# Branch a of a hybrid encoder block as a Strassen product, its operands' sums made beside the projections

## The chip, the cores and the metric

The kernel runs on one core of a Trainium2 chip, as one launch. The metric is device time in microseconds. A core has a matrix engine (PE, with its weight loads shown apart as PEld), a vector engine (DVE), a scalar engine (ACT), GpSimd (POOL) and SyncE (SP); here SP does nothing but issue transfers between DRAM and the core's memories. Each of these works its own list of instructions in order. PSUM is the memory that PE accumulates in; in attention eight banks of 128 x 512 numbers are shared out to fixed uses.

## The reference, cut to what matters

All is float32, with 1024 rows of x (S) and 1024 columns (D).

```
h  = rmsnorm(x);  proj = h @ w_in                      # q, k, v, f, g_b, g_c, hc, two gates
ya = g_b * causal_conv3(g_c * hc)                      # 1024 x 512
yb = softmax(q k^T / 8 + sums of log f, causal) v      # 8 heads of 64: 1024 x 512
ya_d = ya @ w_branch[0]                                # 1024 x 512 by 512 x 1024: "branch a"
yb_d = yb @ w_branch[1]                                # "branch b"
m  = (sigmoid(gate_conv) * ya_d + sigmoid(gate_attn) * yb_d) @ w_out
x  = x + rmsnorm(m);  then a SwiGLU FFN in the same manner
```

The change is to how `ya_d` is computed.

## The kernel before, in words

Every large product is computed in three passes (`mm3`): both operands are split into a high and a low part (`copy` makes the high part on ACT or DVE, `sub` the rest on DVE), and high x high, high x low and low x high are accumulated in PSUM. So one 128 x 128 by 128 x 512 block costs three matmuls. The large products besides branches a and b are already Strassen products: seven block products in place of eight, on sums of the blocks A11 to A22 and B11 to B22 that bear the names S1 to S4 and T1 to T4.

The program's stages, in order: the pre-norm and v (0 to 60 us), 18 projection jobs of 84 matmuls (jobs 0 to 3 make q and k, 4 to 9 what ya is made of, 10 to 17 the gates), attention, branch b, the output projection, the FFN and its down projection. `job` 17 is mixed with the first two steps of attention. In a projection job `strassen` (line 679) makes the seven products; a generator `steps` may be handed to it, and a piece of side work is then done at two places of the job. Before, the side work is `wo_steps`, which makes the sums of w_out's blocks in jobs 7 and 8 and 10 to 15 and spills them to DRAM.

Attention is a loop over steps t = 2 to 22. In each, PE computes scores of two head pairs' blocks (tile `sp`, `step_qk`), multiplies the probabilities of an earlier step with v (`po`, `pv_pair`), and turns probabilities into columns (`tps`, `turn_bank`, copied out as `ptT` by ACT and DVE). Between the two halves of `tps` stands a filler: pieces of branch a, in tile `pba`. Before, `branch_a(d, n)` (twelve matmuls in four units of three) computes the output block of 128 columns d and half n of the rows, and `units` says how many units of three a step gets: 2 in steps 6, 7, 11, 12, 19, 20, 4 in steps 8 to 10, 13 to 16, 21 and 22, 3 in step 17 and 1 in step 18, and none up to step 5. Three blocks of twelve are left for after step 22 (the "tail", 36 matmuls), before branch b (tile `pbb`). A block ends with a multiplication on DVE, `um<-sg,pba`, by its gate tile sg. The operands are w_branch's columns d (`load_wa`, 256 KB, tile `s`, split to `s4h` and `s4l` by `split_wa`) and quarters of ya (`load_ya`, `split_ya`, tiles `yh` and `yl`).

Within attention the program's order is kept on every engine (`strict[0] = engines`). A step's list of `cuts` (splits) is worked off in its middle; its list `at` (loads, divisions) stands at its end. All loads named here are issued by SP. Two chains of other work share SP's list. When the probabilities of a head pair are summed up, `inverse_rows` turns the inverse sums (PE `tr`, DVE copy `rT`), `ri_dram<-rT` stores them to DRAM and `rb<-ri_dram` reads them back spread over partitions, and `divide` multiplies yb by rb on DVE. For the last head pair this happens in two parts, in steps 19 and 22. And `load_kv` and `q_load` bring in the next head pair's k, v and q (tiles `lo`, `v`, `raw`) at the ends of steps 5 and 10; v's buffer is free when the step's `po` has read it.

All instructions of the helpers bear line 76 in the profile, so rows are told apart by their tiles.

## Time and profile before

| | us |
|---|---|
| median of three runs (lowest, highest) | 1316.39 (1316.14, 1318.62) |
| the profiled execution | 1316.02 |
| its span; mean granted clock of PE | 1313.9; 0.999 |
| PE busy | 1305.2 (99% of the span) |
| DVE, ACT, POOL busy | 920.8, 557.1, 188.2 |
| one projection job | 19.1 |
| attention, step 2 to the end of step 22 | 409.2 to 542.8 |
| branch a's tail | 542.8 to 551.1 |

The page gives the busy time of each engine, the span in 40 slices, and the chain of work that ended last. Where a stage of some microseconds matters, the timeline gives single rows: start, duration, engine, line, operation, and tiles (out<-in); SPq rows are the issues of transfers on SP's queue, and the time from issue to landing is listed apart. Steps of attention begin with `sp`: step 11 at 466.98, step 12 at 473.37, step 19 at 520.92, step 20 at 527.48, step 21 at 532.92 (its filler comes first there) and step 22 at 538.56 (likewise).

### The profile page before, as it was taken

How to read it: one execution, taken by the hardware profiler on the slowest of the kernel's cores; microseconds unless marked ns; L12 is line 12 of the kernel's file. 1: busy time of each engine (PE TensorE's matmuls, PEld its weight loads, DVE VectorE, ACT ScalarE, POOL GpSimd, SP SyncE). 2: the span in 40 equal slices, each digit the busy share in tenths (PEclk: the TensorE clock that was granted, in tenths of full speed). 3: DMA queues.
4: the chain of work that ended last, by engine and by line, in shares of the span. 5: the costliest groups of instructions: out<-in, count | busy, mean ns of one | idle time of the engine just before them, and what ended most of it. 6: DMA issues, size and time to landing. Idle time of an engine off the chain costs nothing.

```text
span 1313.9 us, 17693 instructions
## 1 busy us (share of the span) xinstructions
PE 1305.2 (99%) x6695; PEld 1086.7 (83%) x6695; DVE 920.8 (70%) x1314; ACT 557.1 (42%) x869; POOL 188.2 (14%) x349
## 2 busy tenths in 40 slices
PE   9999999999999999999999999999999999999998
PEld 8988888888888888888888888888888888888886
DVE  7885668776656876676677698866766666676674
ACT  7623223243445765613778332322232234444451
POOL 3110001021212221011222122111100110000001
PEclk9999999999999999999999999999999999999999
DMA  6353324565536445674476566533323337966451
GB/s 234 91 159 97 103 87 136 172 209 204 182 121 213 149 135 175 203 250 143 123 243 226 164 205 198 171 112 104 111 74 120 105 112 274 361 215 193 159 169 64
DMA packets 168533, 215.71 MB, mean 164 GB/s; under 512 B 11496, under 2 KB 113968, under 8 KB 168448
## 3 DMA queue, kind: packets, MB, share of 16 engines
q1 hardware_dynamic: 146480, 141.39, 34.4%
q0 software_dynamic: 21952, 73.19, 15.1%
q8 instruction: 52, 0.85, 0.3%
q14 instruction: 33, 0.27, 0.1%
q10 hardware_dynamic: 16, 0.00, 0.0%
HBM read 153.41 MB, written 61.15 MB: 163 GB/s over the span
## 4 chain that ended last, share of the span: by engine, by line
PE 98%; ACT 1%; DVE 1%; issue 0%; DVEq 0%; POOLq 0%; POOL 0%; ACTq 0%
PE b L76 62%; PE pd L76 16%; PE pv L76 3%; PE pbb L76 3%; PE pba L76 3%; PE po L76 2%; PE tps L76 2%; PE sp L76 2%; PE tp L76 1%; PE ma L76 1%; PE mb L76 1%; ACT pt L76 0%; PE spin L76 0%; ACT yh L76 0%; DVE um L76 0%
## 5 line engine op out<-in xcount | busy, mean ns | idle before, releaser
L76 DVE TENSOR_TENSOR c<-c,b 128x512 f32<-128x512 f32 x215 | 146.8, 683 | 95.0 <-PE b L76 87.1
L76 DVE TENSOR_TENSOR lo<-raw,hi 128x1024 fp32r<-128x1024 f32 (+1 forms) x91 | 109.6, 1205 | 78.7 <-PE b L76 63.0
L76 ACT ACTIVATE hi<-raw 128x1024 fp32r<-128x1024 f32 (+1 forms) x98 | 99.6, 1016 | 97.8 <-PE b L76 55.1
L76 ACT ACTIVATE hi<-sx 128x1024 fp32r<-128x1024 f32 x44 | 46.8, 1063 | 217.2 <-PE b L76 191.1
L76 DVE TENSOR_TENSOR lo<-sx,hi 128x1024 fp32r<-128x1024 f32 x44 | 53.8, 1223 | 41.7 <-PE b L76 40.5
L76 PE MATMUL b<-w12h,lo 128*128 128x512 f32 x208 | 80.9, 389 | 0.0
L76 PE MATMUL b<-w12h,hi 128*128 128x512 f32 x204 | 79.4, 389 | 0.0
L76 PE MATMUL b<-w12l,hi 128*128 128x512 f32 x204 | 79.4, 389 | 0.0
L76 PE MATMUL b<-hh,hi 128*128 128x512 f32 x176 | 68.9, 391 | 0.0
L76 PE MATMUL b<-hl,hi 128*128 128x512 f32 x176 | 68.6, 390 | 0.0
L76 PE MATMUL b<-hh,lo 128*128 128x512 f32 x176 | 68.5, 389 | 0.0
L76 DVE TENSOR_TENSOR sx<-raw 128x512 f32<-128x512 f32 x78 | 53.6, 688 | 20.5 <-DMA raw<-in_w_in_dram 12.0
L76 PE MATMUL b<-w,s4h 128*128 128x512 f32 x208 | 64.0, 389 | 0.0
L76 PE MATMUL pd<-hi,lo 128*128 128x512 f32 x160 | 62.2, 389 | 0.0
L76 PE MATMUL pd<-hi 128*128 128x512 f32 x160 | 61.9, 390 | 0.0
L76 PE MATMUL pd<-ghi 128*128 128x512 f32 x148 | 57.6, 389 | 0.0
L76 PE MATMUL pd<-ghi,glo 128*128 128x512 f32 x148 | 57.6, 389 | 0.0
L76 PE MATMUL pd<-glo,ghi 128*128 128x512 f32 x148 | 57.6, 389 | 0.0
L76 POOL DMA_DIRECT2D a_dramA<-um x33 | 17.9, 541 | 276.1 <-DVE um L76 275.5
L76 PE MATMUL b<-hT34h,lo 128*128 128x512 f32 x136 | 52.9, 389 | 0.0
L76 PE MATMUL b<-hT12h,hi 128*128 128x512 f32 x136 | 52.9, 389 | 0.0
L76 PE MATMUL b<-hT12l,hi 128*128 128x512 f32 x136 | 52.9, 389 | 0.0
(457 smaller groups left out, 3576.4 us busy)
## 6 DMA issues: line engine op xcount, KB each, us to landing
raw<-in_w_gate_up_dram SPq DMA_DIRECT2D x52, 512.0 KB, 3.7
raw<-in_w_in_dram SPq DMA_DIRECT2D x35, 512.0 KB, 3.8
a_dramS<-um POOLq DMA_DIRECT2D x44, 256.0 KB, 3.0
a_dramA<-um POOLq DMA_DIRECT2D x33, 256.0 KB, 2.6
sg<-sg_dram SPq DMA_DIRECT2D x32, 256.0 KB, 4.7
graw<-a_dramS SPq DMA_DIRECT2D x14, 512.0 KB, 4.3
sg_dram<-c POOLq DMA_DIRECT2D x24, 256.0 KB, 2.3
raw<-in_w_down_dram SPq DMA_DIRECT2D x11, 512.0 KB, 4.8
```

Of the source, the lines that this page charges most:

```text
L76: ins = getattr(self.engine, name)(*args, **kw)
```

## The change

Branch a becomes a Strassen product of 2 x 2 blocks (512 x 512 columns and rows of the output, contracted over 2 x 256). Each of its seven products P1 to P7 is made in four pieces p of 128 columns; a piece is two blocks deep, six matmuls (`a_chunk`): 28 pieces, 168 matmuls instead of 192. One piece is done in each step 2 to 20 and in step 22, two in step 21 (P5 of p = 3 and P6 of p = 0), and six after step 22: P6 of p = 1, 2, 3 and P7 of p = 1, 2, 3. P1 and P2 of a p share one PSUM accumulation, as do P3 and P4, and P6 and P7 share theirs; when each piece is done DVE (for P1 it is a copy) adds it to a quarter of um, and multiplies a finished quarter by its gate.

The operands' sums (S1 to S4 of the weights, T1 to T4 of ya) and the high and low parts of all operands are made in `wa_steps` and `ya_steps`, as side work of projection jobs 2 to 5 and 10 to 15, and stored by POOL to `wa_dram` and `ya_ops`. In attention they are loaded as they are used, without a split: the weights of each piece (256 KB, one per step in order of use, a ring of five buffers, at the end of a step) and seven operands of ya (1 MB each, in the four homes `HOME`). The loads of k, q and the bias of the first head pair move from job 12 to job 16.

```diff
+    wa_dram = dpool.tile([7, P, 2, 2, NC], F32, name="wa_dram")
+    ya_ops = dpool.tile([7, P, 2, 2, NC], F32, name="ya_ops")
...
+    SUMS_W = ("S3", "S2", "S1", "S4", "A11", "A12", "A22")
+    SUMS_Y = ("T1", "T3", "T2", "T4", "B21", "B22", "B11")
...
+    def wa_steps(k):
...
+        def out(op, t):
+            n = t.shape[1]
+            h = half_tile(w0_tile(tags.popleft()))[:, :n]
+            copy(h, t)
+            strict[0] = ("vector",)
+            sub(t.bitcast(F32R), t, f32(h))
+            strict[0] = ()
+            nc.gpsimd.dma_start(of(op, n)(0), f32(h))
+            nc.gpsimd.dma_start(of(op, n)(1), t)
...
+        sub(s4_[:, 0], a[:, 0], a[:, 1])
+        add(u4[:, 0], a[:, 1], b[:, 1])
+        sub(s4_[:, 1], u4[:, 0], a[:, 0])
+        sub(u4[:, 1], b[:, 0], s4_[:, 1])
+        strict[0] = ()
+        yield
+        out(0, s)
+        yield
+        out(2, u)
...
+    def ya_steps(k):
...
+        sub(t[:, 0], a[:, 1], a[:, 0])
+        sub(u[:, 0], b[:, 1], t[:, 0])
+        strict[0] = ()
+        yield
+        strict[0] = ("vector",)
+        sub(t[:, 1], b[:, 1], a[:, 1])
+        sub(u[:, 1], b[:, 0], u[:, 0])
+        strict[0] = ()
+        yield
+        out(4, b)
+        out(6, a[:, :1])
+        if k == 0:
+            load_rows(ya_rows(1))
+        yield
+        out(0, t)
+        yield
+        out(2, u)
...
+    plans = defaultdict(lambda: [[], []])
+    for first, make in (
+        (((2, 0), (2, 1), (3, 0), (3, 1)), lambda: wa_steps(0)),
+        (((4, 0), (4, 1), (5, 0), (5, 1)), lambda: wa_steps(1)),
+        (((10, 1), (11, 0), (11, 1), (12, 0), (12, 1)), lambda: ya_steps(0)),
+        (((13, 0), (13, 1), (14, 0), (14, 1), (15, 0)), lambda: ya_steps(1)),
+        *(
+            (((j, 0), (j, 1), (j + 1, 0), (j + 1, 1)), lambda k=k: wo_steps(k))
+            for k, j in enumerate((7, 10, 12, 14))
+        ),
+    ):
+        it = make()
+        for j, n in first:
+            plans[j][n].append(it)
...
+            if ij == 16:
...
+                steps=job_steps(plans.pop(ij)) if ij in plans else None,
...
+    HOME = dict(B11="h0", B21="l0", T2="h1", T3="l1", T4="h0", T1="h1", B22="l1")
+    wring = deque()
+
+    def load_y(o):
+        yops[o] = yq.tile([P, 2, 2, NC], F32R, tag=f"y{HOME[o]}", name=f"y{o}", bufs=1)
+        nc.sync.dma_start(f32(yops[o]), ya_ops[SUMS_Y.index(o)])
+
+    def load_w(o, p):
+        if not wring:
+            wring.extend(("s4", "s4h", "s4h", "s4l", "s4l"))
+        tag = wring.popleft()
+        wops[o, p] = wtile(tag, 1 if tag == "s4" else 2, F32R, (P, 4, P))
         nc.sync.dma_start(
-            was[d], w_branch[0, 0][:, d * P : (d + 1) * P].rearrange("(k p) m -> p k m", p=P)
+            f32(wops[o, p]),
+            wa_dram[SUMS_W.index(o)][:, :, :, p * P : (p + 1) * P].rearrange(
+                "p t k c -> p (t k) c"
+            ),
...
+    SEQ = dict(
+        P1=("A11", "B11"), P2=("A12", "B21"), P3=("S2", "T2"), P4=("S3", "T3"),
+        P5=("A22", "T4"), P6=("S1", "T1"), P7=("S4", "B22"),
+    )
+    OPENS = ("P1", "P3", "P5", "P6")
...
+        w, y = SEQ[what]
+        w, y = wops.pop((w, p)), yops[y]
+        kw = {} if what in OPENS else dict(skip_group_check=True)
+        for k in range(2):
             mm3(
-                ps, (wh[:, k, :], wl[:, k, :]), (ya2[n][0][:, k, :], ya2[n][1][:, k, :]),
-                k == 0, k == 3,
+                ps, (w[:, k], w[:, 2 + k]), (y[:, 0, k], y[:, 1, k]),
+                what in OPENS and k == 0, k == 1, **kw,
             )
-            yield None if k < 3 else lambda: mul(um[:, d, ns], sgs[d, n], ps)
-
-
-    FILL = [(d, n) for n in range(2) for d in range(2)]
-    FILL += [(d, n) for d in range(2, 6) for n in range(2)] + [(6, 0)]
-
-    def filler():
-        for d, n in FILL[:-2]:
-            yield from branch_a(d, n, pst, "mb")
-        for d, n in FILL[-2:]:
-            yield from branch_a(d, n, pss, "S")
+        c11, c12, c21, c22 = a_quarters(p)
+
+        def drain():
+            if what == "P1":
+                copy(c21, ps)
+            elif what == "P2":
+                mul(c11, sgs[2 * p, 0], ps)
+            elif what == "P3":
+                add(c12, c21, ps)
+            elif what == "P4":
+                add(c22, c21, ps)
+            elif what == "P5":
+                add(c21, c22, ps)
+                if p < 3:
+                    gate(2 * p + 1, 0)
+            elif what == "P6":
+                add(c22, c22, ps)
+                if p < 3:
+                    gate(2 * p + 1, 1)
+            else:
+                add(c12, c12, ps)
+                gate(2 * p, 1)
...
+    chunks = defaultdict(list)
+    for t, what, p in (
+        (2, "P1", 0), (3, "P2", 0), (4, "P1", 1), (5, "P2", 1), (6, "P1", 2), (7, "P2", 2),
+        (8, "P1", 3), (9, "P2", 3), (10, "P3", 0), (11, "P4", 0), (12, "P5", 0),
+        (13, "P3", 1), (14, "P4", 1), (15, "P3", 2), (16, "P4", 2), (17, "P3", 3),
+        (18, "P4", 3), (19, "P5", 1), (20, "P5", 2), (21, "P5", 3), (21, "P6", 0),
+        (22, "P7", 0),
+    ):
+        chunks[t].append((what, p, pss if what in ("P6", "P7") else pst, "S" if what in ("P6", "P7") else "mb"))
+    A_TAIL = [("P6", 1), ("P6", 2), ("P6", 3), ("P7", 1), ("P7", 2), ("P7", 3)]
+    w_order = deque(
+        (SEQ[what][0], p)
+        for what, p in [c[:2] for t in sorted(chunks) for c in chunks[t]] + A_TAIL
+    )
...
+    for t in range(2, 23):
+        at[t].append(next_w)
+    at[21].append(next_w)
+    for t, o in ((6, "T2"), (7, "T3"), (10, "T4"), (19, "T1"), (19, "B22")):
+        at[t].append(do(load_y, o))
+    for t in (6, 8, 10, 13, 14, 20, 21, 22):
+        at[t].append(next_sg)
...
+    load_y("B11")
+    next_w()
     load_kv(1)
     q_load(1)
+    load_y("B21")
+    for _ in range(2):
+        next_w()
+    for _ in range(4):
+        next_sg()
...
+    done = []
+    for n, (what, p) in enumerate(A_TAIL):
+        done.append(a_chunk(what, p, psm, "mm"))
+        if w_order:
+            next_w()
+        if n < 2:
+            yb_split(0, (2 * n, 2 * n + 1))
+        if n == 2:
+            for m in done[:2]:
+                m()
+            for x in range(2):
+                next_sg()```

On SP, around the end of step 10, the order is now as follows (`s4h` and `s4l` are buffers of the weights' ring, `wa_dram` and `ya_ops` the spilled operands; `yT_4484` is T4):

```order
L76 DMA cb<-c_dram 128x1024 x2
L76 DMA lo<-qk_dram_69 128x1024
L76 DMA v<-v_dram 128x8x128
L76 DMA raw<-qk_dram_69 128x1024
L76 DMA s4h<-wa_dram 128x4x128
L76 DMA yT_4484<-ya_ops 128x2048
L76 DMA sg<-sg_dram_140 128x512
```

T4 and a piece's weights stand behind the loads of the next head pair, where before a raw piece of w_branch and two gate tiles stood. From step 19 on SP had before:

```order
L76 DMA ri_dram_129<-rT 4x128 x2
L76 DMA raw<-in_w_out_dram 128x2x512
L76 DMA rb<-ri_dram_129 64x512 x2
L76 DMA s_5240<-in_w_branch_dram 128x4x128
L76 DMA sg<-sg_dram_140 128x512 x2
L76 DMA raw<-in_w_out_dram 128x2x512
L76 DMA ri_dram_129<-rT 4x128 x2
L76 DMA sg<-sg_dram_133 128x512
L76 DMA rb<-ri_dram_129 64x512 x2
L76 DMA sg<-sg_dram_134 128x512
```

The same stretch of SP in the changed program, from the first `rb` on (`s_5245` are the weights of P6, p = 0, `yT_5247` is T1, `yB_5249` is B22, the `s4l` behind the second `rb` the weights of P6, p = 3):

```order
L76 DMA rb<-ri_dram_131 64x512 x2
L76 DMA s_5245<-wa_dram 128x4x128
L76 DMA yT_5247<-ya_ops 128x2048
L76 DMA yB_5249<-ya_ops 128x2048
...
L76 DMA raw<-in_w_out_dram 128x2x512
L76 DMA ri_dram_131<-rT 4x128 x2
L76 DMA rb<-ri_dram_131 64x512 x2
L76 DMA s4l<-wa_dram 128x4x128
L76 DMA sg<-sg_dram_140 128x512
L76 DMA s_5439<-wa_dram 128x4x128
L76 DMA s4h<-wa_dram 128x4x128 x2
```

The first `rb` now has the operands of P6 behind it, and the second the weights of P6 of p = 3 and of all of P7 that is left. On PE the end of attention is now, from step 20's second half on:

```order
L76 MATMUL pba<-yT_4484,s4l 128x512 x6
L76 MATMUL tps<-ident,pt 128x128 x6
L76 MATMUL pba<-yT_4484,s4l 128x512 x6
L76 MATMUL pba<-yT_5247,s_5245 128x512 x6
L76 MATMUL po<-ptT,v 64x128 x12
L76 MATMUL tps<-ident,rows_970 128x128 x10
L76 MATMUL pba<-yB_5249,s4h 128x512 x6
L76 MATMUL tr<-ident,ri 8x128
L76 MATMUL po<-ptT,v 64x128 x10
L76 MATMUL pba<-yT_5247,s4h 128x512 x6
L76 MATMUL pba<-yT_5247,s4l 128x512 x12
```

Twelve matmuls stood before in the place of step 22's six (`yB_5249`); the last row is P6 of p = 2 and of p = 3.

170 lines of the change are left out of this document (102 added, 68 removed).

## The prediction

> **What bounds the kernel now.** I read the page first (busy times, slices, chain), then the busy time by stage, the waits of TensorE in attention, and last the rows of the SP queue beside the rows of PE and DVE at the places where the change puts loads.
>
> ```profile
> PE 1305.2 (99%) x6695; PEld 1086.7 (83%) x6695; DVE 920.8 (70%) x1314; ACT 557.1 (42%) x869; POOL 188.2 (14%) x349
> GB/s 234 91 159 97 103 87 136 172 209 204 182 121 213 149 135 175 203 250 143 123 243 226 164 205 198 171 112 104 111 74 120 105 112 274 361 215 193 159 169 64
> PE 98%; ACT 1%; DVE 1%; issue 0%; DVEq 0%; POOLq 0%; POOL 0%; ACTq 0%
> ```
>
> PE sets the time: 1305.2 of 1313.9 us are busy, and 98% of the chain is PE. So a matmul that goes is time gained, and anything that makes PE wait is time lost. By stage (the columns are PE, PEld, DVE, ACT and POOL busy, clock, DMA share, GB/s):
>
> ```profile
> 200.00:300.00 100.00, 100.00 (x443) 82.81 (x442) 74.24 (x103) 35.03 (x43) 13.50 (x25) 1.00 0.52 173
> 155.90:175.00 19.10, 19.10 (x87) 15.73 (x86) 13.78 (x21) 5.64 (x7) 0.55 (x1) 1.00 0.35 112
> 308.60:327.70 19.10, 19.10 (x86) 15.83 (x85) 14.52 (x20) 8.53 (x11) 4.87 (x9) 1.00 0.64 225
> 409.20:429.47 20.27, 20.27 (x235) 16.82 (x234) 14.99 (x38) 17.30 (x43) 6.06 (x15) 1.00 0.68 241
> 442.93:479.93 37.00, 36.51 (x339) 30.23 (x339) 26.76 (x59) 24.18 (x57) 7.99 (x18) 1.00 0.40 129
> 532.92:551.13 18.21, 18.21 (x118) 14.66 (x117) 11.55 (x19) 9.49 (x16) 1.56 (x2) 1.00 0.61 197
> ```
>
> The second and third rows are projection jobs, the others attention (steps 2 to 5, 8 to 12, then step 21 to the end of branch a). PE is nowhere idle for long, and DVE has room in all of them.
>
> **The change part by part.**
>
> *Matmuls.* Branch a had 8 x 2 x 4 x 3 = 192 of them and now has 28 x 6 = 168, so 24 go. The row of 387 ns that the tile view gives for one is not its price, since matmuls overlap; their starts are.
>
> ```profile
> 543.17 0.39 PE L76 MATMUL pba<-yl,s4h 128*128 128x512 f32 x1
> 547.05 0.39 PE L76 MATMUL pba<-yh,s4h 128*128 128x512 f32 x1
> ```
>
> These two are 17 matmuls apart: 3.88 us, 0.228 us each (the first stage row gives 100/443 = 0.226). 24 x 0.228 = **-5.5 us**. By place: steps 2 to 5 gain six each (24 more), steps 8 to 10, 13 to 16 and 22 lose six each (48 fewer), step 17 loses three and step 18 gains three. The 36 after the last step stay. So 18 of the 24 (-4.1 us) go before step 22, six (-1.4 us) in it.
>
> *Splits in attention.* 16 subtractions on DVE (0.68 us each) and 16 copies on ACT (0.62) go with the splitting of wa and ya; 16 multiplications of um on DVE become 36 operations. DVE then has four more in all, spread over 21 steps, below its room. What PE can gain is bounded by its waits for ACT and DVE there:
>
> ```profile
> PEld po L76 <- ACT ptT L76: 0.9, 2, 0.6
> PEld po L76 <- ACT pt L76: 0.6, 2, 0.4
> PEld tps L76 <- ACT rows L76: 0.6, 2, 0.4
> PEld tps L76 <- ACT pt L76: 0.4, 2, 0.3
> PEld pba L76 <- DVE um L76: 0.4, 1, 0.4
> ```
>
> The five sum to 2.9 us. Most stand in steps 6 to 8, whose splits go, so at most about 2.3 and at least 0 is won: I take a little more than the middle, **-1.5 us**.
>
> *Sums beside the projections.* 18 half jobs get additions, subtractions and splits on DVE, some 28.6 us in all (7.3 us for each half of wa, 7.0 for each half of ya, worked out from 0.68 us for 128x512 and 1.22 for 128x1024), and 32 stores on POOL. A projection job has 19.1 us of PE and DVE is busy 13.8 and 14.5 in the two quoted. It gets some 3 to 4 more per job: 17.5 to 18. The stored 14.7 MB spread over 10 jobs (190 us) are 77 GB/s more, on 112 to 225 there; a slice of the page moves 361. I cost it at **0**; what hides it is PE's 19.1 us per job, and without that cover it is 0.5 us for each of ten jobs, 5 us (a rival below).
>
> *Loads in attention.* Before, 4 MB of wa and ya came in; now 7 MB of wa sums (28 of 256 KB) and 7 MB of ya sums (7 of 1 MB). The amount is no problem at 129 to 241 GB/s, but all of them are issued by SP, which works its queue in order, and three stand behind an issue that has to wait. That is where I expect the loss.
>
> *T4, for P5(0) in step 12.* As the order rows show, it is behind v and raw of the next head pair.
>
> ```profile
> 470.19 0.37 SPq L76 DMA_DIRECT2D v<-v_dram  x1
> 470.61 1.62 SPq L76 DMA_DIRECT2D raw<-qk_dram  x1
> DMA to landing us min/median/max: 6.5/6.5/6.5
> ...
> 477.59 0.48 PE L76 MATMUL pba<-yh,s4h 128*128 128x512 f32 x1
> ```
>
> The v load went out at 470.19, 3.2 us into step 11 (its buffer is read by PE's po of that step), raw at 470.61, and raw took 6.5 us (third row), to 477.1. Step 12's filler is reached at 477.59. T4 is issued after raw and the weights, at about 473, and has 1 MB behind raw's 512 KB: with 6.5 to 8 us it lands at 479.5 to 481, with the 4.9 of a row below it is in time within 0.3. I take 479.6: **+2.0 us** (0 to 3.5).
>
> *T1, for P6(0) in step 21.* It is issued in step 19, behind the load of rb, and rb's buffers are read by the divisions of yb on DVE.
>
> ```profile
> 529.19 1.28 DVE L76 TENSOR_TENSOR yb<-yb,rb 128x512 f32<-128x512 f32 x2
> 530.51 1.09 SPq L76 DMA_DIRECT2D rb<-ri_dram  x2
> 533.59 0.68 DVE L76 TENSOR_TENSOR s4l<-s,s4h 128x512 fp32r<-128x512 f32 x1
> 534.19 0.68 DVE L76 TENSOR_TENSOR um<-sg,pba 128x512 f32<-128x512 f32 x1
> 534.39 0.40 PE L76 MATMUL pba<-yh,s4h 128*128 128x512 f32 x1
> wh<-wt_dram SPq DMA_DIRECT2D x1, 1024.0 KB, 4.9
> w<-w_dram POOLq DMA_DIRECT2D x2, 1024.0 KB, 6.6
> ```
>
> rb goes out at 530.51, when both divisions are done. The change puts P5(1)'s addition and gate ahead of them on DVE (0.6 us each, from 533.59 to 534.19): 531.7. Then rb takes 1.09 and the weights of P6(0) 0.5, so T1 goes out at 533.3. A transfer of 1 MB lands in 4.9 to 6.6 us; with 5.7 that is 539.0. PE reaches P6(0) at 534.39, the seventh filler matmul of step 21. **+4.6 us** (2.6 without the delay on DVE and with 4.9; 6 at the other end). Queued behind it on PE are po and tps of that step, so all of what follows is late by as much.
>
> The Trainium skill ("DMA: Bandwidth & Descriptors", section "Anatomy of one DMA — SWDGE (gpsimd) path") fits a DMA's time as 2.0 us plus bytes over 436 GB/s, for GpSimd's path. By that estimate 1 MB takes 4.4 us, T1's wait is 3.3 and the whole sum 1323.5 us instead of 1324.8; the two rows above are longer and I go by them.
>
> *The weights of P6(3), after step 22.* They are issued in step 22 behind the way of the row sums of the last head pair: PE's tr, DVE's rT, the store ri_dram, and its reading back as rb.
>
> ```profile
> 538.56 0.48 PE L76 MATMUL pba<-yh,s4h 128*128 128x512 f32 x1
> 541.40 0.68 DVE L76 TENSOR_TENSOR s4l<-s,s4h 128x512 fp32r<-128x512 f32 x1
> 543.13 0.27 DVE L76 COPY rT<-tr 8x128 f32<-8x128 f32 x1
> 543.43 0.60 SPq L76 DMA_DIRECT2D ri_dram<-rT  x2
> 546.67 1.09 SPq L76 DMA_DIRECT2D rb<-ri_dram  x2
> 547.85 4.55 SPq L76 DMA_DIRECT2D sg<-sg_dram  x3
> SPq L76 <- DMA ri_dram<-rT: 6.5, 4, 3.3
> s<-in_w_branch_dram SPq DMA_DIRECT2D x8, 256.0 KB, 4.5
> DMA to landing us min/median/max: 2.8/2.8/2.8
> ```
>
> SP stores at 543.43, waits for the store until 546.67 (the row of waits has it as its longest, 3.3 us), issues rb, and is free at 547.85. Now DVE has two more operations of um ahead of rT and one s4l less, +0.6: SP is free at 548.4, 9.85 us after step 22 began (538.56). 256 KB land in 2.8 us at best (last row, the s of 534.30) and 4.5 at the median; with the load of rb still going I take 5.0: 14.85 after the step's start. The 24 matmuls from P6(3) on take 24 x 0.228 = 5.5, so branch a ends 20.3 us after the step's start, where it ended 551.13 - 538.56 = 12.57 after it: **+7.8 us** net, the six matmuls saved in step 22 already in it (5.6 with 2.8 us, 9.9 at 7). Without the weights being late P6(3) would be reached 5.6 us after the step's start, so the wait itself is 9.2 us. Two shorter waits ahead of it (step 21's rows behind P5(3)'s addition, P6(1) behind the addition of P7(0), which holds its PSUM bank) are swallowed by it. Branch b behind it has its operands earlier, counted from its own start, so nothing follows from there.
>
> The same section of the Trainium skill says that DMA engines do not wait on semaphores, the issuing sequencer does, before it dispatches. That speaks against this change, and the trace agrees: SP issued nothing from 544.5 to 546.67.
>
> *Sum.* -4.1 - 1.5 + 0 + 2.0 + 4.6 + 7.8 = +8.8 us. The profiled execution lasted 1316.0 us (span 1313.9 and 2.1 around it), 0.4 below the median of the runs: 1316.0 + 8.8 = **1324.8 us**. The low ends give -4.1 - 2.3 + 2.6 + 5.6 = +1.8 (1317.8), the high ends -4.1 + 3.5 + 6 + 9.9 = +15.3 (1331).
>
> **Rivals.**
>
> *The loads are in time (faster).* If SP's waits end early enough, as when rb no longer holds the loads up, or the loads land before PE comes, only the gain is left: -5.5 - 1.5 = -7.0, 1309.0 us. For it speaks that PE hardly waits for DMA before; against it that T1 would have to land 1.1 us after its issue at 533.3, and P6(3)'s weights before they are issued. It decides if both are issued over 5 us earlier than I read. 0.10.
>
> *One late load, not three (no change).* If the last load is in time but T4 and T1 are late, -5.5 - 1.5 + 2.0 + 4.6 = -0.4 (1315.6); if only the last is late, -5.5 - 1.5 + 9.2 = +2.2 (1318.2). For it: each price hangs on one place in a queue. 0.12.
>
> *The sums stall the projections too (slower still).* Two jobs of DVE at 18 us of 19.1 leave 1 us; if c's accumulations are late behind a block of sums, PSUM banks are not free and PE waits 0.5 us in ten jobs: 1329.8 us. Against it: no wait of PE in the projections before. 0.13.
>
> My own forecast has the rest, 0.65, with a range of its own of 1317.8 to 1331.
>
> **How the numbers follow.** A measurement can tell about 0.2% (2.6 us) from no change. Faster is the first rival, 0.10, and a little of the second; the second's two cases lie within 2.6 us, and so does the low edge of my forecast; the rest is slower. Faster 0.11, same 0.13, slower 0.76. The range is 1316.5 to 1331.5: it takes in both bounds of the sum, one case of the second rival and the third rival, and leaves out the first rival and the other.
>
> **What would show it.** Between step 2 and step 20 PE should take 4.1 us less, but for a wait of some 2 us ahead of pba in step 12, put down to the 1 MB yT. In step 21 PE should stand some 4 to 5 us between the sixth and the seventh filler matmul, for the second 1 MB yT, issued right behind rb. After step 22 PE should stand about 9 us ahead of the third chunk of the tail, for weights issued right behind the last rb. The projection jobs should still take 19.1 us with DVE at 15 to 18. If PE has no wait over 2 us in step 21 and after step 22, the forecast is wrong and the time is near 1309; if the projections grow, the third rival holds.

## The result and the profile after

The changed kernel takes 1355.69 us (median of four runs, 1352.99 to 1356.86), the kernel before beside it 1316.79 (four runs, 1316.14 to 1318.62): a ratio of 1.029, 95% interval 1.027 to 1.031. It is slower, as forecast, but by 38.9 us where 8.4 were forecast, and outside the range of 1316.5 to 1331.5. The profiled execution lasted 1352.99 us, 37.0 more than the one before.

Two rows of the page that answer to those shown of before are the busy times and the mean rates in the 40 slices:

```profile
PE 1309.4 (97%) x6671; PEld 1086.7 (80%) x6671; DVE 947.3 (70%) x1352; ACT 564.1 (42%) x875; POOL 210.6 (16%) x381
GB/s 227 100 166 179 188 140 172 171 210 239 253 225 183 277 181 191 193 278 221 110 190 245 203 164 181 193 133 86 117 101 117 87 116 226 362 243 198 162 164 63
```

PE has 24 matmuls fewer, as counted, and is nevertheless busy for 4.2 us longer: some of its matmuls are slow. It now stands idle for 41.8 us of the span (before 8.7). In the projections no slice exceeds 253 GB/s, where the highest of the kernel has 362, so the page alone doesn't show why.

Marks in the PE rows of both traces divide the 37 us. One is the last product ahead of the last projection job, before and now:

```profile
384.64 0.39 PE L76 MATMUL b<-hT34h,lo 128*128 128x512 f32 x1
409.67 0.39 PE L76 MATMUL b<-hT34h,lo 128*128 128x512 f32 x1
```

**25.0 us are lost before attention,** 0.4 of them before the first projection job. From that mark to the start of branch b's last product it takes 209.78 us before and 221.52 now: **+11.7 us** (forecast: +8.8 in attention and the tail). Behind branch b it takes 0.5 us more.

Attention first. The middle of it, steps 2 to 11 and 12 to 19, by the view of busy time in stretches (columns as in the prediction: PE, PEld, DVE, ACT and POOL busy, clock, DMA share, GB/s), before:

```profile
409.20:473.37 64.17, 63.59 (x634) 52.61 (x633) 48.49 (x108) 47.86 (x110) 15.90 (x37) 1.00 0.49 165
473.37:527.48 54.11, 54.07 (x506) 45.04 (x506) 36.57 (x89) 33.62 (x80) 11.77 (x27) 1.00 0.48 157
```

and after:

```profile
434.23:498.41 64.18, 64.18 (x638) 53.42 (x638) 42.41 (x98) 44.17 (x103) 15.53 (x37) 1.00 0.62 211
498.41:547.74 49.33, 48.53 (x483) 40.39 (x482) 36.52 (x89) 32.00 (x77) 11.29 (x27) 1.00 0.57 192
```

118.28 us have become 113.51, 4.8 less, with T4's wait in it. Then come the waits, here those of PE behind that mark (waited in all, times, longest):

```profile
PE pba L76 <- DMA s4l<-wa_dram: 6.5, 1, 6.5
PE pba L76 <- DVE um L76: 3.5, 2, 2.0
PE pba L76 <- DMA yT<-ya_ops: 2.8, 1, 2.8
PE tps L76 <- DVE um L76: 1.1, 1, 1.1
PE pba L76 <- DVE ptT L76: 0.8, 1, 0.8
```

The first is the weights of P6(3), the third T1; the two on `um` are additions that free a PSUM bank. The last names DVE, but it stands ahead of T4's first product and is gone when T4 is loaded earlier (e4, below), so I count it as T4's. All stand where the prediction put them, or beside it. The rows of SP and PE at the end of attention:

```profile
552.09 1.12 SPq L76 DMA_DIRECT2D rb<-ri_dram  x2
553.91 0.62 SPq L76 DMA_DIRECT2D yT<-ya_ops  x1
559.54 0.78 PE L76 MATMUL pba<-yT,s 128*128 128x512 f32 x2 [2.75 <-DMA yT<-ya_ops]
570.88 0.60 SPq L76 DMA_DIRECT2D ri_dram<-rT  x2
574.21 1.12 SPq L76 DMA_DIRECT2D rb<-ri_dram  x2
575.43 0.68 SPq L76 DMA_DIRECT2D s4l<-wa_dram  x1
580.98 1.65 PE L76 MATMUL pba<-yT,s4l 128*128 128x512 f32 x3 [6.45 <-DMA s4l<-wa_dram]
```

T1 goes out behind `rb` and PE takes it up 5.6 us after its issue. The weights of P6(3) go out behind the second `rb`, 4.6 us after the store, and PE takes them up 5.55 us later. Behind both waits the clock is down (the first two rows) and then full again (the third):

```profile
559.50:564.00 4.50, 4.46 (x30) 3.47 (x30) 0.00 (x0) 0.00 (x0) 0.00 (x0) 0.62 0.99 332
581.00:583.00 2.00, 2.00 (x5) 1.61 (x6) 0.69 (x1) 0.00 (x0) 0.00 (x0) 0.50 1.15 346
585.00:587.00 2.00, 2.00 (x11) 1.65 (x10) 1.14 (x2) 0.00 (x0) 0.00 (x0) 1.00 1.03 408
```

Now the projections. Jobs 13 and 15, which took 19.1 us each before:

```profile
311.10:341.60 30.50, 21.69 (x85) 17.10 (x85) 16.59 (x23) 10.49 (x15) 7.48 (x13) 0.89 0.62 219
361.60:390.50 28.90, 21.13 (x86) 16.69 (x85) 16.52 (x22) 8.35 (x11) 5.82 (x10) 0.94 0.77 263
```

The two have lost 21.2 of the 25.0 us; job 4 lost 2.1 and job 14 about 0.9. PE stands in six places: 2.10 us at 153.7, 6.79 at 316.8, 2.79 at 336.0, 1.03 at 347.3, 5.34 at 367.3 and 3.21 at 384.4 (each from the start of a matmul to the start of the next). These are two rows of PE's waits, none of which stood there before:

```profile
PE b L76 <- DVE lo L76: 12.0, 3, 6.4
PE b L76 <- DVE c L76: 6.9, 3, 2.8
```

`lo` is the low part of the next projection operand; `c` is the accumulation of products on DVE, for which PE waits at 153.7, 336.0 and 384.4. DVE is named, but it is not busy: it has 16.6 us of work in the 30.5 us of job 13. One has to go back one step more. Around the longest wait, rows of POOL, SP, DVE and PE:

```profile
300.06 1.28 POOL L76 DMA_DIRECT2D ya_ops<-rows  x2
...
304.69 0.71 POOL L76 DMA_DIRECT2D ya_ops<-yh  x1
...
303.60 1.56 SPq L76 DMA_DIRECT2D rows<-ya_dram  x2
306.08 1.20 SPq L76 DMA_DIRECT2D raw<-in_w_in_dram  x1
319.07 0.69 DVE L76 TENSOR_TENSOR sx<-raw 128x512 f32<-128x512 f32 x1 [11.27 <-issue]
323.60 0.79 PE L76 MATMUL b<-hT12h,lo 128*128 128x512 f32 x1 [6.41 <-DVE lo L76]
```

The same load and its reader in the kernel before:

```profile
302.03 19.41 SPq L76 DMA_DIRECT2D raw<-in_w_in_dram  x3
306.50 0.69 DVE L76 TENSOR_TENSOR sx<-raw 128x512 f32<-128x512 f32 x1 [1.14 <-DMA raw<-in_w_in_dram]
```

A block of w_in that DVE took up 4.5 us after its issue is now taken up 13.0 us after it; DVE stands idle for 11.3 us ahead of that (the row names no releaser, but in later kernels a wait of the same kind bears the transfer's name, below). The load is also issued later counted from its job, 5.0 us ahead of it where it was 6.6: on SP it stands behind the load of ya's rows. And the transfers in these microseconds:

```profile
300.00:303.00 3.00, 3.00 (x15) 2.45 (x14) 3.00 (x5) 1.53 (x3) 2.54 (x4) 1.00 1.08 399
323.60:326.00 2.40, 2.40 (x6) 1.91 (x7) 2.40 (x4) 2.24 (x4) 0.54 (x1) 0.50 0.55 150
```

The 16 transfer engines are full from 300 to 317 us (mean share 1.04 and 372 GB/s, in stretches of 3 us 299 to 403 GB/s): five stores of ya's sums go out within 5 us, and ya's rows, w_out's block and w_in's block come in. At 318 us the share is down to 0.02, and at 319.07 DVE takes the block up. Most of this burst falls in job 12, which loses nothing by it and whose mean is 298 GB/s (182 before); job 13, where PE stands, has a mean of 219 in the view above, less than the 225 it had before. The second row is the clock when PE goes on. The second pause of job 13 has another owner, ACT:

```profile
333.50 1.06 ACT L76 ACTIVATE h<-r 128x1024 fp32r<-128x1024 f32 x1 [7.50 <-DMA w_dram<-h]
334.46 1.05 ACT L76 ACTIVATE hi<-sx 128x1024 fp32r<-128x1024 f32 x1
```

`h<-r` is side work for w_out; its buffer is free when an earlier store of `h` has landed. Behind it in ACT's order stands `hi<-sx`, the high part of the next projection operand. In DVE's order side work (`r<-r,h`) that needs this copy stands ahead of an accumulation of `c`, for which PE waits.

### The profile page after: what moved, and what is told of

Read it like the earlier page. It is cut to its first block, busy times and chain, and to the rows that moved or that the text cites. A ratio compares the mean times of both kernels' runs of the same rounds, so it can differ in the third digit from the quotient of the medians.

```text
span 1351.2 us, 17833 instructions
## 1 busy us (share of the span) xinstructions
PE 1309.4 (97%) x6671; PEld 1086.7 (80%) x6671; DVE 947.3 (70%) x1352; ACT 564.1 (42%) x875; POOL 210.6 (16%) x381
## 4 chain that ended last, share of the span: by engine, by line
PE 69%; DMA 2%; DVE 1%; issue 1%; SPq 0%; DVEq 0%; POOLq 0%; ACT 0%; POOL 0%; ACTq 0%
PE b L76 39%; PE pd L76 16%; PE pbb L76 3%; PE pba L76 3%; PE po L76 3%; PE tps L76 2%; PE sp L76 2%; PE ma L76 1%; PE mb L76 1%; PE tp L76 1%; DMA raw<-in_w_in_dram 0%; DMA s4l<-wa_dram 0%; DMA yT<-ya_ops 0%; DVE lo L76 0%; DMA ri_dram<-rT 0%
## 5 line engine op out<-in xcount | busy, mean ns | idle before, releaser
L76 DVE TENSOR_TENSOR c<-c,b 128x512 f32<-128x512 f32 x215 | 146.7, 683 | 71.1 <-PE b L76 69.5
L76 DVE TENSOR_TENSOR lo<-raw,hi 128x1024 fp32r<-128x1024 f32 (+1 forms) x91 | 109.6, 1205 | 66.0 <-PE b L76 49.5
L76 ACT ACTIVATE hi<-raw 128x1024 fp32r<-128x1024 f32 (+1 forms) x98 | 99.5, 1015 | 91.1 <-PE b L76 46.0
L76 ACT ACTIVATE hi<-sx 128x1024 fp32r<-128x1024 f32 x44 | 46.7, 1061 | 166.8 <-PE b L76 141.6
L76 DVE TENSOR_TENSOR sx<-raw 128x512 f32<-128x512 f32 x78 | 53.7, 689 | 58.1 <-DMA raw<-in_w_in_dram 26.9
L76 PE MATMUL b<-w12h,lo 128*128 128x512 f32 x208 | 80.9, 389 | 0.0
L76 PE MATMUL b<-w12h,hi 128*128 128x512 f32 x204 | 79.4, 389 | 0.0
L76 PE MATMUL b<-w12l,hi 128*128 128x512 f32 x204 | 79.4, 389 | 0.0
L76 DVE TENSOR_TENSOR lo<-sx,hi 128x1024 fp32r<-128x1024 f32 x44 | 53.8, 1223 | 33.9 <-PE b L76 29.2
L76 PE MATMUL b<-hh,hi 128*128 128x512 f32 x176 | 68.9, 392 | 0.0
L76 PE MATMUL b<-hl,hi 128*128 128x512 f32 x176 | 68.5, 389 | 0.0
L76 PE MATMUL b<-hh,lo 128*128 128x512 f32 x176 | 68.5, 389 | 0.0
L76 PE MATMUL b<-hT12h,lo 128*128 128x512 f32 x136 | 55.0, 405 | 12.1 <-DVE lo L76 12.0
L76 PE MATMUL b<-w,s4h 128*128 128x512 f32 x208 | 64.0, 389 | 0.0
L76 PE MATMUL pd<-hi,lo 128*128 128x512 f32 x160 | 62.3, 389 | 0.0
L76 PE MATMUL pd<-hi 128*128 128x512 f32 x160 | 61.9, 390 | 0.0
L76 POOL DMA_DIRECT2D a_dramA<-um x33 | 17.9, 543 | 276.7 <-DVE um L76 275.8
L76 PE MATMUL b<-hT34h,hi 128*128 128x512 f32 x136 | 53.3, 392 | 6.9 <-DVE c L76 6.9
L76 PE MATMUL pd<-ghi 128*128 128x512 f32 x148 | 57.6, 390 | 0.0
L76 PE MATMUL pd<-glo,ghi 128*128 128x512 f32 x148 | 57.6, 389 | 0.0
L76 PE MATMUL pd<-ghi,glo 128*128 128x512 f32 x148 | 57.6, 389 | 0.0
L76 PE MATMUL b<-hT12l,hi 128*128 128x512 f32 x136 | 54.1, 398 | 0.0
```

Of the source, the lines that this page charges most:

```text
L76: ins = getattr(self.engine, name)(*args, **kw)
```

## The experiments

**Theory A** after the result: the loss before attention comes from the sums made and stored beside the projections, and the rest from late loads in attention. The two are separate. **Rival**: the loss is elsewhere, as in the moved loads of k and q.

**e1: sums without their use.** Attention and branch a as before, the sums made and spilled all the same.

```diff
-    chunks = defaultdict(list)
...
+    fill = filler()
+    units = {6: 2, 7: 2, 8: 4, 9: 4}
```

> The sums beside the projections and their spilling are kept; attention and branch a are those of the kernel before, which do not read the sums (so the spilled operands are unused). In the changed kernel's profile the first row of step 2 of attention starts at 434.2 us, before at 409.2: 25 us are lost before attention. Theory (the sums cost the projections 25 us, whatever attention does): 1316.5 + 25 = 1341 us, with pauses of PE in jobs 4, 13 and 15 at the same places. Rival (the projections are slow only because the loads for the Strassen pieces were pulled ahead into them): about 1317 us.

Measured: 1340.04 us, ratio 1.0175 (1.0159 to 1.0190), +23.3. The pauses are those of the changed kernel (5.06 us at 315.9, 5.87 at 364.3, 3.78 at 382.3). Theory A holds for this part: the sums alone cost 23 us. The moved loads of k and q still stand in job 16 here; e8 below speaks to them.

**e4: loads early, the other part alone.** The loads of T4, T1 and B22 one or two steps earlier, the weights' ring two pieces further ahead, and the last `rb` issued behind the tail's weights.

```diff
-    for t, o in ((6, "T2"), (7, "T3"), (10, "T4"), (19, "T1"), (19, "B22")):
+    for t in (12, 14):
+        at[t].append(next_w)
+    for t, o in ((6, "T2"), (7, "T3"), (9, "T4"), (17, "T1"), (18, "B22")):
...
+            if part == 1:
+                late.append(back)      # rb is issued behind the first weights of the tail
```

> The changed kernel with attention's loads moved on SP's list: T4 at the end of step 9 (was 10), T1 at 17 and B22 at 18 (were 19), the ring of weights two pieces further ahead from step 14 on, and the last reading back of rb behind the tail's weights. Theory (T1 and the weights of P6 of p = 3 are late because of where they stand; each pause of PE also costs some 2 us at half the granted clock behind it: 0.62 in 559.5 to 564 and 0.50 in 581 to 583 us): the pause of 3.2 us in step 21 and that of 6.8 us in the tail go, with 2.2 us of slow clock behind each; 1355 - 14 = 1341 us (1338 to 1345). Rival (the 1 MB and 256 KB loads are late because the transfer engines are full at that place, share 1.04 in 555.1 to 559.5, so loads put elsewhere are late as well): 1350 to 1357 us.

Measured: 1341.05 us, ratio 1.0192 (1.0166 to 1.0218), 14.6 less than the changed kernel and in the theory's range. PE's waits in attention that are left:

```profile
PE pba L76 <- DVE um L76: 3.5, 2, 2.0
PE tps L76 <- DVE um L76: 1.1, 1, 1.1
```

The three waits for transfers are gone, with the slow matmuls behind them; from the mark ahead of the last projection job to that at the end of branch b it takes 207.92 us, 1.9 less than before. So the three late loads together cost 14.6 us by the medians and 13.6 between the marks, and they hung on their places in SP's order. All were moved at once, so no single one is priced by this run.

**e2: an eighth of the stores.** The stores of the sums write 16 of 128 partitions, attention reads other stored data of the same size. Issues, additions and splits are unchanged.

```diff
-            nc.gpsimd.dma_start(of(op, n)(0), f32(h))
+            nc.gpsimd.dma_start(of(op, n)(0)[:SPILL], f32(h)[:SPILL])     # SPILL = 16, all stores likewise
-        nc.sync.dma_start(f32(yops[o]), ya_ops[SUMS_Y.index(o)])
+        nc.sync.dma_start(f32(yops[o]), wt_dram[0][:, 0].rearrange("t p x c -> p t x c"))
```

> The changed kernel, but each store of a spilled operand writes 16 of its 128 partitions (1.8 MB in place of 14.7), with the same instructions, waits and order; attention reads other stored data of the same size in their place, so branch a's values are not the reference's. Theory (in jobs 12 to 15 the transfer engines are full: share 0.97 to 1.08 and 300 to 405 GB/s in the rows from 300 to 318 us, so the 512 KB of w_in issued at 306.1 are only used at 319.1): the pauses in the projections go, but for less than 4 us; step 2 starts at 410 to 413 us, and the whole takes 1329 to 1333. Rival A (SP's list: the loads of ya's rows wait until the rows' tile is free, and w_in's loads stand behind them) and rival B (DVE and ACT have too much to do in order) do not hang on the bytes: step 2 still starts near 434, the whole near 1354.

Measured: 1342.8 us, ratio 1.0194 (1.0177 to 1.0211). The first product of attention's scores comes at 407.09 us (420.87 in the changed kernel, 395.84 before): 14 of the 25 us go with the bytes, 11 stay. Neither expectation met. The total fell by only 12.9 us, since attention, which now loads other data, takes longer in this run. The reader of job 13's block and the copy on ACT now:

```profile
309.86 0.69 DVE L76 TENSOR_TENSOR sx<-raw 128x512 f32<-128x512 f32 x1 [3.73 <-issue]
...
323.68 1.06 ACT L76 ACTIVATE h<-r 128x1024 fp32r<-128x1024 f32 x1 [6.88 <-DMA w_dram<-h]
```

The transfer engines are full here too, but only until 309 us (share 0.93 to 1.05, then 0.13). The block (issued at 302.81) is taken up as that ends, after 7.1 us instead of 13.0, and the pause of 6.79 us is gone. ACT's wait is hardly shorter (6.9 against 7.5), and PE stands 3.35 us behind it.

**e3: ya's and w_branch's rows loaded by POOL.** If SP's order alone were the cause, moving these loads off SP would end it.

```diff
-            nc.sync.dma_start(rows4[:, n], rows_)
+            nc.gpsimd.dma_start(rows4[:, n], rows_)
```

> The changed kernel, with the loads of the rows of w_branch and ya, from which the sums are made, issued by POOL and not by SP. SP then has no wait for the rows' tile ahead of w_in's loads. Theory (full transfer engines): the same bytes at nearly the same time, so at most 3 us less: 1350 to 1357 us, and the pauses in jobs 13 and 15 stay over 3 us each. Rival A (SP's list): w_in's loads are on time, the pauses go, 1329 to 1335 us.

Measured: 1363.23 us (two runs), ratio 1.0351 (1.0331 to 1.0372), slower by 7.5 than the changed kernel. Neither time expected was met, and pauses of over 3 us stayed. POOL works in order too, and its stores now wait behind the loads: `rows<-ya_dram` goes out at 310.23 behind a wait for a store, and the pause there is 8.04 us. The block of w_in was issued at 311.94 with no load of rows ahead of it on SP, and was taken up 14.4 us later. SP's order is not the cause by itself.

**e5: w_out's first copy in a tile of its own.** e2 with the `h` of `wo_steps` in another buffer, so that it doesn't wait for the store.

```diff
-            h = flat(w0_tile("h0")).rearrange("p (a b) -> p a b", a=2)
+            h = flat(w0_tile("h0")) if n or not k else z_tile("wh", F32R)
```

> As the run with an eighth of the spilled bytes, and in jobs 10 to 15 the first of w_out's two copies (h<-r) goes to another tile than the one whose store to w_dram is still under way. In that run 11 us stayed in the projections, with pauses of PE of 3.35 us at 325.6 and 3.99 at 369.2; before each, ACT stands for 6.9 and 7.7 us ahead of h<-r for the store w_dram<-h, with the split hi<-sx of the next job's weights queued behind it. Theory (that wait in ACT's order is what is left): both pauses go with the half clock behind them, 1342.8 - 8 = 1335 us (1332 to 1338). Rival (DVE's work itself is too long, or the moved loads of k, q and the bias): 1341 to 1344.

Measured: 1340.82 us, ratio 1.0183 (1.0165 to 1.0201), 2.0 less than e2 and outside both expectations; the single runs of e2 and e5 lie 3.6 and 6.1 us apart. In the profiled executions attention begins 4.7 us earlier than in e2 (402.41), so 4.7 us is the figure of one execution of each. The two pauses behind ACT's wait (3.35 and 3.99 us in e2) are gone. A new one of 3.82 us stands at 374.3, where a block of w_in is taken up 9.6 us after its issue, although only an eighth of the sums' bytes is stored; here the row puts DVE's wait down to the transfer. Of the 25 us, 6.6 remain.

**e8: no sums of ya.** e1 without `ya_steps`, whose results e1 doesn't use.

```diff
-        (((10, 1), (11, 0), (11, 1), (12, 0), (12, 1)), lambda: ya_steps(0)),
-        (((13, 0), (13, 1), (14, 0), (14, 1), (15, 0)), lambda: ya_steps(1)),
```

> As the run with the sums alone (attention as before), but without ya's sums: what is left are w_branch's sums in jobs 2 to 5 and the loads of k, q and the bias in job 16 in place of 12. Theory (ya's sums, their stores and what these hold up are the loss): only the pause in job 4 stays, 1316.5 + 2 = 1318 to 1320 us. Rival (the moved loads hold up the weights in jobs 14 to 16): 1324 to 1330 us.

Measured: 1321.91 us, ratio 1.0033 (1.0021 to 1.0045), 18 less than e1 and between the two expectations. Left are two pauses: 2.04 us at 153.4, and 2.75 at 202.1 in job 7, where no sums of branch a are made and which the changed kernel does not have. So ya's sums, which share jobs 10 to 15 with w_out's, cost some 18 of the 23 us, and w_branch's sums 5 at most. That suggests that it is the two kinds of side work on top of each other that is dear, but no run puts ya's sums in jobs of their own. No pause is left in jobs 14 to 16, though the loads of k and q still stand in job 16: by themselves they cost nothing there.

**e7: is the slow clock a term of its own?** 27 matmuls, whose results are not read, between P6(2) and P6(3).

```diff
+        if n == 2:
+            for _ in range(9):
+                mm3(idle_ps, (iw[:, 0], iw[:, 2]), (iy[:, 0, 0], iy[:, 1, 0]), True, True)
```

> The changed kernel with 27 matmuls more into a spare bank ahead of P6 of p = 3, where PE stands for 6.84 us; nothing reads them. Theory (after a pause PE's clock is at half for some 3 us: the profile grants 0.70, 0.50 and 0.77 in 574.5 to 585 us): with PE kept busy the granted clock stays 1.00 and the 24 matmuls from there on take 5.5 us in place of 7.4; the time is 2 us less than the changed kernel's (1351 to 1355). Rival (those matmuls are slow for another reason, as late weights): 7.4 us and no gain, clock 0.5 again.

Measured: 1352.91 us (two runs, 1350.53 and 1355.29), against 1355.69. The rows behind the pause, which is 2.46 us now:

```profile
583.00:585.00 2.00, 0.01 (x1) 0.01 (x1) 0.00 (x0) 0.00 (x0) 0.35 (x1) 1.00 1.10 357
585.00:587.00 2.00, 2.00 (x9) 1.62 (x10) 1.00 (x2) 0.00 (x0) 0.40 (x1) 1.00 1.15 357
```

The clock stays at 1.00. From PE's resumption to the start of branch a's last matmul it takes 5.36 us (584.99 to 590.35), in the changed kernel 7.14 (580.98 to 588.12), of which 0.56 are two matmuls of branch b between: 1.2 us of that wait's cost were the clock. In this run the weights also came 1.75 us later, counted from `tr`, so the total doesn't show it.

**Towards a version that gains.** The next five runs change where the side work stands, all with attention's loads as in e4. e6 spreads it (w_out's in jobs 6 to 11 and 13 to 15, one operand of ya per half job) and gives P5(3) a bank of its own:

```diff
-        (((13, 0), (13, 1), (14, 0), (14, 1), (15, 0)), lambda: ya_steps(1)),
+        (((13, 1), (14, 0), (14, 1), (15, 0), (15, 1), (16, 0)), lambda: ya_steps(1)),
...
-            for k, j in enumerate((7, 10, 12, 14))
+                ((6, 0), (6, 1), (7, 0), (7, 1)),
+                ((8, 0), (8, 1), (9, 0), (9, 1)),
+                ((10, 0), (10, 1), (11, 0), (11, 1)),
+                ((13, 1), (14, 0), (14, 1), (15, 0)),
```

> A mend of both halves. Projections: w_out's sums are moved to jobs 6 to 11 and 13 to 15 (from 7, 8 and 10 to 15), ya's sums stay in jobs 10 to 16 but store one operand pair in each half job. Attention: the early loads of the run with 1341 us; P5 of p = 3 gets a bank that no earlier piece holds, and its addition is done after the copies of the last rows. Theory (the projections lose by bursts of transfers and by ACT's wait for a store, which spreading takes away; attention alone is worth -7): 1316.5 - 6.4 + 2 to 5 for what is left in jobs 4 to 16: 1311 to 1316 us. Rival (the engines for transfers are too full on the mean of jobs 10 to 15, so spreading doesn't help): 1325 to 1335.

Measured: 1334.19 us, ratio 1.0146 (1.0124 to 1.0168), in the rival's range. From mark to mark attention and branch b take 205.75, 4.0 less than before. The projections have still lost 20.5: in place of two dear jobs there are five pauses, of 1.4 to 4.6 us.

e9 leaves out more meetings (w_branch's second half later, `h` of w_out in a buffer that is free longer, ya's rows and the first loads of k and q later):

```diff
-        (((4, 0), (4, 1), (5, 0), (5, 1)), lambda: wa_steps(1)),
+        (((4, 1), (5, 0), (5, 1), (6, 0)), lambda: wa_steps(1)),
...
-        h = flat(w0_tile("h0")).rearrange("p (a b) -> p a b", a=2)
+        h = rows4[:, 2].bitcast(F32R) if k < 2 else z_tile("wh", F32R)
```

> The mended version once more (1334 us), with more room around what ACT and SP had to wait for in it: the second half of w_branch's sums starts half a job later, when its rows have landed (ACT stood 5.4 us for them at 146.5 in the changed kernel, with hi<-sx behind); w_out's first stored tile is another than its first copy's; ya's second rows are loaded one half job after the stores that free their tile; k, q and the bias are loaded in job 16's first half. Behind attention the additions of P6 stand ahead of the splits of yb on DVE. Theory (what is left in the projections are waits of ACT's and SP's lists for single loads and stores, since the engines for transfers are idle half the time): the projections lose 3 to 8 us in place of 20, and the time is 1312 to 1319 us. Rival (the bytes themselves: 14.7 MB more written and 4 read in jobs 2 to 16): 1325 us or more.

Measured: 1325.15 us, ratio 1.0049 (1.0030 to 1.0067), the rival again. The largest pause left in the projections is 4.21 us in job 16, into which the loads of k, q and the bias had moved, and here the row names the transfer:

```profile
365.80 0.34 SPq L76 DMA_DIRECT2D rows<-c_dram  x1
366.24 0.40 SPq L76 DMA_DIRECT2D raw<-in_w_in_dram  x1
376.77 0.69 DVE L76 TENSOR_TENSOR sx<-raw 128x512 f32<-128x512 f32 x1 [8.36 <-DMA raw<-in_w_in_dram]
```

From issue to use it takes 10.5 us. Another pause, of 4.8 us, stands in the tail of branch a.

e10 and e11 put the last side work of w_out and ya into other halves of jobs 13 to 16. e10 also changes the order of POOL's loads for the output projection, so that fewer bytes move at the end of attention; e11 leaves that order, gives the last weights of the tail a buffer of their own and lets POOL issue the bias rows of the first head pair:

```diff
+    strict[0] = ("gpsimd",)                          # e10: these loads in the order as written
     load_sum([t[:, 1] for t in w12], 1, 1)
     load_sum([t[:, 0] for t in w12], 0, 0)
...
+        if (o, p) == ("S4", 3):                      # e11
+            wops[o, p] = yb_pool.tile([P, 4, P], F32R, tag="wx", name="wx", bufs=1)
+            q = nc.sync if j else nc.gpsimd
+            q.dma_start(cbs[key], c_dram[2 * j + e].partition_broadcast(P))
```

> The version of 1325 us with two further moves. POOL loads w_out's A12 sums ahead of its A22 sums, so that the two loads w<-w_dram of 1 MB no longer go out at 545 and 551 us beside the last weights of branch a (issued 551.0, used 560.3: PE stood 4.8 us, and 2 us of slow clock follow). And the last of w_out's sums starts a job earlier, ya's second half half a job later, so that fewer stores fall between 357 and 377 us, where 360 to 410 GB/s were moved and the next weights took 10.4 us to land (PE stood 4.2 us). Theory (both pauses are transfers that meet others): 1325 - 6.7 - 3 to 6 = 1312 to 1316 us. Rival (the bytes only move to where they hurt as much): 1320 to 1326.

> The version of 1333 us with two moves in place of the one that failed. There the loads of w_out's A22 sums, put behind those of A12, came late for the output projection (PE stood 9.1 us at 612.5); the old order is back, and the last weights of branch a, whose lateness that move had taken away, are loaded in step 19 into a tile of their own. And the two loads of the bias rows for head pair 0, the first of which stood on SP ahead of job 16's weights and waited until 369.35 for a store of ya's sums (the weights behind it went out at 369.86, PE stood 5.9 us), are issued by POOL. Theory: 1332.7 - 9.1 - 3 for the slow clock - 5.9 - 2 = 1313 us (1311 to 1317), the kernel before within a few us. Rival (the pause in job 15 comes from the transfers' time, not from SP's order): 1318 to 1322.

Measured: e10 1332.71 us, ratio 1.0115 (1.0098 to 1.0132); e11 1319.78 us (eleven runs), ratio 1.0017 (1.0008 to 1.0026). e10 met neither expectation, e11 its rival. In e10 the tail's pause is gone, but the pause in job 16 grew to 5.85 us, and now a load that POOL issues behind these is late for the output projection:

```profile
612.68 0.76 POOL L76 DMA_DIRECT2D wl<-wt_dram  x1 [5.77 <-issue]
621.61 0.80 PE L76 MATMUL b<-wl,raw 128*128 128x512 f32 x1 [8.63 <-DMA wl<-wt_dram]
```

e11 has +7.8 us before attention (three pauses of 1.1, 2.0 and 2.8 us) and -4.3 from the mark there to that at the end of branch b. It is the best of the versions, and not faster than before.

e12, last, takes the second load of ya's rows out of SP's order, where it stood ahead of w_in's block; some of ya's sums come to stand elsewhere by it:

```diff
-            load_rows(ya_rows(1))
+            load_rows(ya_rows(1), nc.gpsimd)
```

> e11's kernel with the second load of ya's rows issued by POOL instead of SP, the sum o6 of ya made ahead of o4, and the sums of ya(1) placed as three groups in job 14's second half, one in each half of job 15 and one at job 16's first. e11 ran 1319.78 us with 7.8 us left in the projections, of which pauses of 1.96 us in job 13 and 2.79 us in job 15 and half-speed matmuls behind the second. Theory (what is left is SP's in-order row loads that stand ahead of the input's loads): both pauses shrink below 1.2 us, the first product of attention's scores comes 2 to 4 us earlier than in e11, and the time is 1315 to 1318 us. Rival (what is left is the added bytes, which slow whatever load is under way): the pauses only change places, and the time is 1318 to 1322 us.

Measured: 1320.95 us, ratio 1.0023 (1.0012 to 1.0034): the rival. The pause of 1.97 us in job 14 grew to 3.54, that of 2.79 in job 16 fell to 2.24 (the expectation has them in jobs 13 and 15). Ya's rows don't stand ahead of job 14's load any more (w_out's block does, as it did before the change), it is issued 6.4 us ahead of its job, and it is late all the same:

```profile
323.68 15.91 SPq L76 DMA_DIRECT2D raw<-in_w_in_dram  x2
334.71 0.69 DVE L76 TENSOR_TENSOR sx<-raw 128x512 f32<-128x512 f32 x1 [8.02 <-DMA raw<-in_w_in_dram]
```

11.0 us from issue to use, with the transfer engines full (share 0.84 to 1.10) up to 332.7, two stretches of which are:

```profile
323.70:326.70 3.00, 3.00 (x15) 2.49 (x14) 1.82 (x2) 1.07 (x1) 0.30 (x1) 1.00 0.94 279
326.70:329.70 3.00, 3.00 (x15) 2.49 (x14) 0.00 (x0) 0.63 (x1) 1.38 (x3) 1.00 1.10 361
```

POOL had issued stores of ya's sums at 320.0, 321.1 and 322.3, and issued `rows<-ya_dram` at 326.4. The load is late with no wait on SP ahead of it; which of the transfers under way delays it (the stores ahead, or the load of rows behind) was not separated.

## Why the prediction was wrong, point by point

**The direction and the places in attention were right.** Steps 2 to 19 were to take 4.1 us less by matmuls and 1.5 by waits, with 2.0 for T4: 3.6 less in all. They take 4.8 less, and T4's wait is 0.8, so without it they take 5.6 less, as forecast. T4's wait was 1.2 us shorter than priced.

**T1: +4.6.** T1 was issued 6.2 us after step 20 began (forecast 5.8) and taken up 5.6 later (5.7). PE stands 1.77 us for P5(3), whose bank waits for P5(2)'s addition, and then 3.15 for T1; less the 0.23 of an ordinary matmul each, 4.5. So far the size holds, though a part of it shows ahead of P5(3). But from step 20 to step 22's filler it takes 7.6 us more than before: 1.7 are slow matmuls behind the wait, and 1.1 is the wait of `tps` for P5(3)'s addition, which the prediction had swallowed by the next wait; it lies ahead of step 22, on whose start that next wait hangs, and is added.

**P6(3): +7.8 net.** From step 22's filler (566.46) to the issue of the weights it takes 9.0 us (forecast 9.85), to PE's resumption 14.5 (14.85). The wait of P6(1), 2.32 us, is swallowed, as said. Branch a's end is 8.8 us later against its step than before; the 1.0 more is the next point.

**A term was missing: the clock.** I priced the 24 matmuls behind this wait at 0.228 us each, 5.5 us. They took 6.8, and e7 gives 1.2 of that back. With the 1.7 behind T1 it is 3.0 us in attention. Behind the pauses of 6.79 and 5.34 us in the projections it is 3.7 (0.50 for 2.4 us and 0.52 for 2.0 behind the first, 0.50 and 0.73 for 2.0 each behind the second). PE's busy time should have fallen by 5.5 us and rose by 4.2; 6.7 of these 9.7 us are in the four places, the rest I did not locate. The Trainium skill ("TensorE: Matmul & The Clock Gate", section "Part 1: The HAM clock gate (the "warmup" mystery)") says that the half clock is the default and that some 3.4 us of work release it. By an estimate from these figures each such wait costs another 1.7 us or so; the 0.50 here and the return to 1.00 within 4 us agree.

So attention and branch a came to +11.6 where +8.8 was forecast: 1.2 less up to step 20, 3.0 more from there to step 22, 1.0 more behind it. Without the 25.0 us the profiled execution would have taken 1328.0, 3.2 above the forecast and inside the range; it is by luck that T4's shorter wait hides a part of the missing clock.

**The step that failed is "Sums beside the projections ... I cost it at 0; what hides it is PE's 19.1 us per job".** It cost 25.0 us (23.3 alone, in e1). Three things were wrong in it:

- The bytes were averaged: 14.7 MB over ten jobs gave 77 GB/s on top of 112 to 225, against a slice of 361. But the sums leave in bursts, five stores within 5 us, and meet the loads of ya's rows and of w_out and w_in in the same stretch: 372 GB/s at a share of 1.04 for 17 us. The job that held most of it lost nothing, and the next one, with a mean of 219, stood still. What matters is the one load that PE needs next; it took 13.0 us instead of 4.5. With an eighth of the stored bytes 14 of the 25 us were gone (e2).
- The cover was counted for DVE only. Side work puts its copies into ACT's list and its loads into SP's, both in order. A copy that waits for a store, or a load that waits for a buffer, holds what PE needs next. Freeing one such copy of its store brought 4.7 us net, in one execution of each kernel (e5 against e2).
- The side work of ya fell upon that of w_out in the same jobs. The part that had jobs of its own (w_branch) cost 5 us at most, the other some 18 (e8 against e1). That the meeting of the two made it dear is the likely reading, not a shown one.

The rival "the sums stall the projections too" (0.13) named the right place, and half of the mechanism: three of the six pauses, 6.9 us of waiting, are for c's accumulations, as it says. But DVE was not full, as the rival had it; it had 16.6 us of work in job 13, where the prediction had 17.5 to 18 in 19.1, and was idle for 13.9. In jobs 13 and 15 c was late because side work ahead of it in DVE's order waited for a copy on ACT, and that for a store. The two longest pauses are of another kind, late loads, and the price of 0.5 us in each of ten jobs is a fifth of what came, mostly in two jobs.

**The other rivals.** Loads in time (1309.0): in e4 they are, and attention and branch b are then 1.9 us shorter than before, 4.3 in e11, of the 7.0 hoped for; in e4 the three waits on additions that are left take most of the rest, 4.6 us. That the whole would be faster came true in no version tried. One late load, not three: all three were late.

**The range** (1316.5 to 1331.5) took in the low and high ends of the sum and, as a rival, 5 us for the projections. Their 0.5 us per job had no row behind them. A bound was to be had from a row: the block of w_in is taken up 4.5 us after its issue, and in the changed kernel a job loses several us, not a half, where it comes two to three times as late.

**What stays open.** In the best version 7.8 us remain in the projections (1.3 of it ahead of the first job). e12 shows that they move with the order of the transfers and don't vanish; whether a slower, evenly spread spill would hide them was not tried. In e5, with an eighth of the stored bytes and the copy freed, 6.6 of the 25 us are left. Whether ya's stores are worse for meeting the moved loads of k, q and the bias in job 16 was not separated. In the versions tried attention and branch b gained 4.3 us at most, so the projections would have to lose less than that.

## What to carry to other kernels

Work that is put "beside" a stage that is bound by PE has to be checked in stretches of a few microseconds, not by the mean of the stage: look for a load that PE needs soon, at the time when the added stores leave, and add what they move there to what is moved already. List every engine whose in-order queue the side work enters, and ask of each instruction what it waits for and what stands behind it. A long wait of PE may be followed by matmuls at half speed, here 1.3 to 2.2 us more each time. Every pause of 4.2 us and more that was looked at had them behind it, and of those between 2.5 and 4.0 some had them and some had not.
